# A Mamba-2 scan layer on one Trainium2 core: masked products in pairs with the decay matrix moving, and x of groups 2 and 3 turned with the last result

## The chip, the cores and the metric

The kernel runs on one core of a Trainium2 chip. The core has five engines with an instruction stream each: TensorE (PE, matrix products; its weight loads are shown apart as PEld), VectorE (DVE), ScalarE (ACT), GpSimd (POOL) and SyncE (SP, which only issues DMAs). Every engine works through its own instructions in the order of the program, and waits at semaphores for the others. The metric is the device time of one execution in microseconds (us). Before the change it is 1010.27 us, the median of three runs (1009.69 to 1010.57).

## The reference

The program is a decoder trunk of two layers for 256 tokens and a width of 1024: each layer is a SwiGLU, a token mixer and a second SwiGLU, each with a layer norm behind it. The mixer of the first layer is sparse attention, that of the second a Mamba-2 scan. Only the scan is touched:

```python
SSM_INNER = 2048; SSM_HEAD_DIM = 64; SSM_HEADS = 32; SSM_GROUPS = 4; SSM_STATE = 128; SSM_CHUNK = 128

def ssd_scan(x, dt, a, b_in, c_in):
    ...
    xdt = (x * dt[..., None]).reshape(bsz, nc, q_len, g_n, r_n, p_dim)
    a_cs = cumsum of (dt * a) within a chunk of 128 tokens
    seg = a_cs[..., :, None] - a_cs[..., None, :]
    decay = jnp.exp(jnp.where(tri, seg, -jnp.inf))
    cb = jnp.einsum('bclgn,bcsgn->bcgls', cm, bm)
    y_diag = jnp.einsum('bcgrls,bcsgrp->bclgrp', cb[:, :, :, None] * decay, xdt)
    ...
    return (y_diag + y_off).reshape(bsz, seq, n_h, p_dim)

y = ssd_scan(...) + xs * d_skip
yz = y * silu(z)                       # then an RMS norm within each group of 512 columns
return yz @ w_out
```

So there are 2 chunks (t = 0, 1) of 128 tokens, and 4 groups (g = 0 to 3) of 8 heads with 64 columns. For each chunk, group and head a 128 x 128 matrix, the product of `cb` and `decay`, is multiplied by a 128 x 64 block of `xdt`: 64 such products, the "masked products" of the title. All is float32.

## The kernel before, in words

**Weights.** All weights stream from HBM in units of 128 x 1024 numbers. Each unit is split into a high half (`wh`, a cast on ACT, lines 324 and 326) and a low half (`wl`, a subtraction on DVE, lines 351 and 354; for a few units a negative copy on ACT, line 332, and an adding DMA from POOL's queue, line 333), and a projection is three products of halves (`mm3`, lines 539 to 541). `W.pump(1)` prepares one unit further ahead, up to ten; its `wh` goes to ACT where it stands, its `wl` to DVE at the next `lows()`.

**The scan.** `ssd` runs, for g = 0 to 3, one pass of the loop over groups. The long projections stand in it as *fillers*, `f[0]`, `f[1]` and so on, which keep PE busy while the other engines work on the scan: `xs_tile` (24 products of 256 columns: x of the next group, then its convolution on ACT and DVE and a silu on ACT), `z_half` (12 products of 512 columns: half of a gate z, at its end a silu on ACT) and `out_piece` (12 products of 512 columns: the layer's output, into the four accumulator banks). Between the fillers, written out by hand in one order for all engines, stand the steps of the scan:

- `decay_load` (a DMA from POOL's queue, 512 KB), `decay_seg` (DVE), `decay_exp` (ACT, two exponentials of 1024 columns) and `decay_cb` (DVE) make M, the masked decay matrix of 8 heads, for a chunk and group.
- `x_tok` turns x of a group to tokens x columns (four transposes on PE) and multiplies it by dt and by the skip weight (two DVE instructions); `x_end` makes the block for the carry between chunks.
- `diag` does the 8 masked products of a chunk and group. M is the stationary operand, the 64 columns of x move, and the result stands as tokens x columns in a PSUM bank.
- `carry` (PE, then two DVE instructions) takes chunk 0 to chunk 1; `gate` (two DVE instructions) adds the skip part and multiplies by silu(z); `square` (ACT), `root` (POOL) and `norm` (ACT) normalise; `y_tr` turns the result back for the output projection (four transposes on PE, the high half `yH` on ACT, line 535, the low half `yL` on DVE, line 536).

ACT holds one set of function tables at a time; the exponentials need another than the silus, so each pair of `decay_exp` stands between two `ACT_TABLE_LOAD`. `late` and `flush()` put the silu of a convolution off to the next one.

**Banks.** Of PSUM's eight banks, two are called ptr, two pmm, and four (acc00, acc01, acc10, acc11) are the output's accumulators from group 2 on and lent out until then. Before the change, chunk 0's products use ptr, chunk 1's use acc11 in groups 0 and 1 and ptr in groups 2 and 3. The turned x of chunk 0 uses acc11 (pmm in group 3), that of chunk 1 uses ptr.

Of the kernel before, what the change touches and what calls it, by code (L numbers as in the profile page):

```python
# [11 lines left out]
F32 = mybir.dt.float32  # L12
# [400 lines left out]
def trunk_kernel(ctx: ExitStack, tc: tile.TileContext, widths, forms, x, ln_g, ln_b, wts, kvg, convp,  # L413
                 dt_bias, a_log, d_skip, norm_g, out):
    nc = tc.nc
# [10 lines left out]
    def nm(s):  # L426
        cnt[0] += 1
        return f"{s}_{cnt[0]}"
# [4 lines left out]
    def f2(s):  # L433
        return wk.tile([128, 512], F32, name=nm(s), tag="f2", bufs=9)
# [13 lines left out]
    def pmm():  # L448
        return psum.tile([128, 512], F32, name=nm("pmm"), tag="pmm", bufs=2)
# [11 lines left out]
    def ptr():  # L461
        return psum.tile([128, 512], F32, name=nm("ptr"), tag="ptr", bufs=2)
# [915 lines left out]
    def ssd(xT, u, ln_i):  # L1378
# [104 lines left out]
        def decay_load(t, g):  # L1483
            M[t, g] = f4("M")
            nc.gpsimd.dma_start(M[t, g], scr[t:t + 1, g * 8:(g + 1) * 8, :].rearrange("o h l -> o (h l)")
                                .to_broadcast([128, 1024]))
# [4 lines left out]
        def flush():  # L1491
            while late:
                nc.scalar.activation(*late.pop(0), AF.Silu)
# [48 lines left out]
        def decay_seg(t, g):  # L1542

            mv = M[t, g].rearrange("p (h l) -> p h l", h=8)
            nc.vector._custom_dve(TENSOR_ADD_SAT, out=mv, in0=mv, s0=0.0, s1=-3e38,
                                  in1=nacs[t][:, g * 8:(g + 1) * 8][:, :, None].to_broadcast([128, 8, 128]))

        def decay_exp(t, g):
            nc.scalar.activation(M[t, g], M[t, g], AF.Exp)
# [4 lines left out]
                                 .to_broadcast([128, 8, 128]))  # L1554

        yT = {}
        y, xd, xe, ss = {}, {}, {}, {}

        def x_tok(t, g):

            if t:
                pt = ptr()
            elif g < 3:
                pt = psum.tile([128, 512], F32, name=nm("pxt"), tag="acc11", bufs=1)
            else:
                pt = pmm()
            for i in range(4):
                nc.tensor.transpose(pt[:, i * 128:(i + 1) * 128], xsT[g][i][:, t * 128:(t + 1) * 128], ident)
            y[t], xd[t] = f2("xdt"), f2("xtok")
            nc.vector.tensor_mul(hv(y[t]), hv(pt), hb(dt[:, t * 32:(t + 1) * 32], g))  # L1570
            nc.vector.tensor_mul(hv(xd[t]), hv(pt), hb(dsk, g))
# [3 lines left out]
            nc.vector.tensor_mul(hv(xe[g]), hv(y[0]), hb(dend, g))  # L1575

        def diag(t, g):
            m = M.pop((t, g))
            py = psum.tile([128, 512], F32, name=nm("py"), tag="acc11", bufs=1) if t and g < 2 else ptr()
            for h in range(8):  # L1580
                nc.tensor.matmul(py[:, h * 64:(h + 1) * 64], m[:, h * 128:(h + 1) * 128],
                                 y[t][:, h * 64:(h + 1) * 64], start=True, stop=True)
            return py

        def carry(g):

# [5 lines left out]
        def gate(t, g, py):  # L1592
            nc.vector.tensor_add(y[t], py, xd[t])
            nc.vector.tensor_mul(y[t], y[t], zs[g][:, t * 512:(t + 1) * 512])
# [78 lines left out]
        decay_exp(1, 0)  # L1673
        W.lows()
        u += 4
        py = {}
        for g in range(SG):
            if g < 2:
                f = [lambda i=i: xs_tile(g + 1, i, u + i) for i in range(4)]
                f += [lambda t=t, i=i: (z_half(g + 2, t, i, u + 4), W.pump(1)) for t in range(2) for i in range(2)]  # L1680
            elif g == 2:
                x3 = [lambda i=i: xs_tile(3, i, u + 2 * i) for i in range(4)]
                o0 = [lambda i=i: out_piece(i, u + 2 * i + 1) for i in range(4)]
                f = [x3[0], x3[1], o0[0], x3[2], o0[1], x3[3], o0[2], o0[3]]
            else:
                f = [lambda i=i: out_piece(4 + i, u + i) for i in range(6)]
            f[0]()
            if g:
                x_tok(0, g)
                x_tok(1, g)  # L1690
            else:
                decay_cb(0, 0)
                decay_cb(1, 0)
            x_end(g)
            f[1]()
            f[2]()
            py[0] = diag(0, g)
            gate(0, g, py[0])
            carry(g)
            if g < 3:  # L1700
                decay_load(0, g + 1)
            f[3]()
            square(0)
            root(0)
            py[1] = diag(1, g)
            gate(1, g, py[1])
            if g < 3:
                decay_load(1, g + 1)
            f[4]()
            norm(0)  # L1710
            square(1)
            root(1)
            if g < 3:
                decay_seg(0, g + 1)
            f[5]()
            y_tr(0, g)
            norm(1)
            if g < 3:
                decay_seg(1, g + 1)
                f[6]()  # L1720
                flush()
                y_tr(1, g)
                decay_exp(0, g + 1)
                decay_exp(1, g + 1)
                f[7]()
                decay_cb(0, g + 1)
                decay_cb(1, g + 1)
                W.lows()
                u += 8
# [56 lines left out]
```

## Time and profile before

The page shows one profiled execution. "Busy" is the time in which an engine had an instruction running; matmuls are pipelined, so the distance between two starts is a better measure on PE than the length of one.

| | before |
|---|---|
| median of three runs | 1010.27 us |
| span of the profiled execution, first to last instruction | 1009.0 us |
| PE busy | 999.1 us (99%) |
| PEld busy | 845.8 us (84%) |
| DVE busy | 905.3 us (90%) |
| ACT busy | 662.0 us (66%) |
| POOL busy | 109.8 us (11%) |
| granted TensorE clock, mean | 0.999 |

The time of the profiled execution itself isn't listed apart from its span; the median of the runs stands 1.3 us above the span. A row of a timeline gives the start in us from the beginning of the span, the length, the engine, the line of the kernel, the operation with its output and inputs, the shape, and how many equal instructions are merged into the row. In brackets stands for how long the engine had been idle, and what ended that. A float32 product stands in the timeline as two passes, so 8 masked products are a row of 16.

### The profile page before, as it was taken

The page shows a single profiled execution, that of the slowest core. Times are in us where ns is not written, and L with a number is a line of the kernel's source. Part 1 is how long each engine was busy: PE and PEld are TensorE (multiplying, and loading weights), DVE is VectorE, ACT ScalarE, POOL GpSimd, SP SyncE. Part 2 cuts the span into 40 slices and gives each one's busy share as a digit, 9 for nine tenths or more (in the row PEclk, how much of TensorE's full clock was granted, in tenths as well). Part 3 has the DMA queues.
Part 4 walks back from the last instruction along what each step waited for, and adds up shares of the span by engine and source line. Part 5 has one row for each costly group of instructions (what it writes and reads, how often), then busy time and mean ns, then how long its engine had stood idle before and what let it go on. Part 6 is the DMA issues. An engine that isn't in the chain of part 4 may idle for free.

```text
span 1009.0 us, 14555 instructions
## 1 busy us (share of the span) xinstructions
PE 999.1 (99%) x5273; PEld 845.8 (84%) x5273; DVE 905.3 (90%) x1224; ACT 662.0 (66%) x968; POOL 109.8 (11%) x149
## 2 busy tenths in 40 slices
PE   9999999999999999999999999999999999999997
PEld 6888888898788888888888888999888888888886
DVE  7899999888898999999899998788989978899996
ACT  6676776476755767764576776486876645676670
POOL 0010110100000101100010110150221100010100
PEclk9999999999999999999999999999999999999999
DMA  9799889551754998995499889457765754699981
GB/s 347 224 289 284 240 254 334 195 172 57 245 173 126 274 280 241 260 390 183 123 281 288 243 253 357 168 179 241 222 215 181 235 191 136 170 265 285 289 254 42
DMA packets 66055, 231.69 MB, mean 230 GB/s; under 512 B 8112, under 2 KB 9136, under 8 KB 65984
## 3 DMA queue, kind: packets, MB, share of 16 engines
q1 hardware_dynamic: 54288, 189.84, 51.7%
q0 software_dynamic: 11120, 40.41, 21.7%
q8 instruction: 41, 0.67, 0.3%
q10 hardware_dynamic: 576, 0.52, 0.2%
q14 instruction: 30, 0.25, 0.1%
HBM read 193.48 MB, written 1.08 MB: 193 GB/s over the span
## 4 chain that ended last, share of the span: by engine, by line
PE 94%; DVE 3%; DMA 1%; issue 1%; POOL 0%; ACT 0%; DVEq 0%; POOLq 0%; SPq 0%
PE pmm L539 12%; PE pmm L540 12%; PE pmm L541 12%; PE acc L539 10%; PE acc L541 10%; PE acc L540 10%; PE ptr L539 2%; PE ptr L541 2%; PE ptr L540 2%; PE pxs L539 2%; PE pxs L541 2%; PE pxs L540 2%; PE pmm L705 1%; PE ptr L705 1%; PE ptr L795 1%; PE pmm L685 1%
## 5 line engine op out<-in xcount | busy, mean ns | idle before, releaser
L354 DVE TENSOR_TENSOR wl<-raw,wh 128x1024 fp32r<-128x1024 f32 (+3 forms) x424 | 495.5, 1211 | 14.6 <-ACT wh L326 14.1
L326 ACT CAST wh<-raw 128x1024 fp32r<-128x1024 f32 (+2 forms) x431 | 428.8, 1043 | 91.8 <-DVE raw L293 51.1
L539 PE MATMUL acc<-wh,hH 128*128 128x512 f32 (+1 forms) x352 | 138.1, 392 | 0.0
L541 PE MATMUL acc<-wh,hL 128*128 128x512 f32 (+1 forms) x352 | 136.5, 388 | 0.0
L540 PE MATMUL acc<-wl,hH 128*128 128x512 f32 (+1 forms) x352 | 136.3, 387 | 0.0
L539 PE MATMUL pmm<-wh,xT 128*128 128x512 f32 (+2 forms) x304 | 119.2, 392 | 0.0
L541 PE MATMUL pmm<-wh,xT 128*128 128x512 f32 (+2 forms) x304 | 116.9, 384 | 0.0
L540 PE MATMUL pmm<-wl,xT 128*128 128x512 f32 (+2 forms) x304 | 116.7, 384 | 0.1
L266 POOL DMA_DIRECT2D raw<-raw x64 | 55.8, 877 | 490.3 <-DVE raw L293 260.4
L541 PE MATMUL pmm<-wh,xf 128*128 128x512 f32 x256 | 99.6, 389 | 0.0
L539 PE MATMUL pmm<-wh,xf 128*128 128x512 f32 x256 | 99.6, 389 | 0.0
L540 PE MATMUL pmm<-wl,xf 128*128 128x512 f32 x256 | 99.6, 389 | 0.0
L541 PEld LDWEIGHTS acc<-wh,hL 128*128 128x128 f32 x352 | 66.1, 188 | 13.7
L293 DVE TENSOR_TENSOR raw<-raw,raw 128x1024 f32<-128x1024 f32 x64 | 77.0, 1218 | 0.2
L540 PEld LDWEIGHTS acc<-wl,hH 128*128 128x128 f32 x352 | 66.2, 188 | 12.9
L539 PEld LDWEIGHTS acc<-wh,hH 128*128 128x128 f32 x352 | 66.1, 188 | 12.8
L541 PEld LDWEIGHTS pmm<-wh,xT 128*128 128x128 f32 x304 | 57.0, 188 | 11.9 <-DVE xT L536 0.5
L540 PEld LDWEIGHTS pmm<-wl,xT 128*128 128x128 f32 x304 | 57.2, 188 | 11.0 <-DVE wl L354 0.8
L539 PEld LDWEIGHTS pmm<-wh,xT 128*128 128x128 f32 x304 | 57.1, 188 | 10.0
L541 PEld LDWEIGHTS pmm<-wh,xf 128*128 128x128 f32 x256 | 48.0, 188 | 10.0
L539 PEld LDWEIGHTS pmm<-wh,xf 128*128 128x128 f32 x256 | 48.0, 188 | 10.0
L540 PEld LDWEIGHTS pmm<-wl,xf 128*128 128x128 f32 x256 | 48.0, 188 | 10.0
(321 smaller groups left out, 1784.6 us busy)
## 6 DMA issues: line engine op xcount, KB each, us to landing
raw<-in_wts_dram SPq DMA_DIRECT2D x338, 512.0 KB, 5.9
raw<-raw POOLq DMA_DIRECT2D x64, 512.0 KB, 5.4
M<-scr POOLq DMA_DIRECT2D x8, 512.0 KB, 6.0
lng<-in_ln_g_dram SPq DMA_DIRECT2D x6, 512.0 KB, 5.5
lnb<-in_ln_b_dram SPq DMA_DIRECT2D x6, 512.0 KB, 5.9
wl<-raw POOLq DMA_DIRECT2D x5, 512.0 KB, 5.5
raw<-in_wts_dram SPq DMA_DIRECT2D x4, 408.0 KB, 5.4
out_dram<-x SPq DMA_DIRECT2D x4, 256.0 KB, 2.0
```

What stands on the lines that cost most here:

```text
L266: self.nc.gpsimd.dma_start(self.raw[r], self.raw[other], accum_op=ALU.add)
L293: self.nc.vector.tensor_add(self.raw[r], self.raw[r], self.raw[other])
L326: nc.scalar.copy(h[:, c:c + n], raw[:, c:c + n])
L354: self.nc.vector.tensor_sub(lo[:, s], raw[:, s], h[:, s].bitcast(F32))
L539: nc.tensor.matmul(ps, lh, rh, start=first, stop=False, skip_group_check=on)
L540: nc.tensor.matmul(ps, lh, rl, start=False, stop=False, skip_group_check=on)
L541: nc.tensor.matmul(ps, ll, rh, start=False, stop=last, skip_group_check=on)
L685: nc.tensor.matmul(ps, a, b[:, c], start=k == i == 0, stop=k == DK - 1 and i == 2)
L705: nc.tensor.matmul(ps, H[:, k * 128:(k + 1) * 128], xT.HL[:, k, :], start=k == 0, stop=False)
L795: nc.tensor.transpose(v[:, i, t * 128:(t + 1) * 128], hs[t][:, i * 128:(i + 1) * 128], ident)
```

## The change

The masked products swap their operands. The 64 columns of x become the stationary operand and M moves, 128 columns at a time; two heads are written to the two halves (partitions 0 to 63 and 64 to 127) of the same 128 columns of a bank. The result stands as columns x tokens, so ACT copies it to SBUF (`ydT`) and `back`, a new step, turns it with four transposes on PE into a ptr bank, from which `gate` reads. Between `diag` and `back` stands one filler. For that, chunk 0's `diag` goes one filler ahead in groups 1 to 3, and `gate` one filler back in group 0; chunk 1's `diag` goes ahead to stand right behind chunk 0's `back`, and the carry behind it. In group 0 the steps up to the first `y_tr` stand one filler later than before. Chunk 1's products use pmm in groups 2 and 3. The loads of the next decay matrix move ahead with the `diag` that frees their tile. `x_tok` of the next group goes to the end of the pass in groups 0 and 1 (so x of the second and third group is turned behind the last `y_tr`), and in group 0 `decay_exp` and the last filler go ahead of the second `y_tr`.

```diff
         def diag(t, g):
+
             m = M.pop((t, g))
-            py = psum.tile([128, 512], F32, name=nm("py"), tag="acc11", bufs=1) if t and g < 2 else ptr()
-            for h in range(8):
-                nc.tensor.matmul(py[:, h * 64:(h + 1) * 64], m[:, h * 128:(h + 1) * 128],
-                                 y[t][:, h * 64:(h + 1) * 64], start=True, stop=True)
+            if not t:
+                py = ptr()
+            else:
+                py = psum.tile([128, 512], F32, name=nm("py"), tag="acc11", bufs=1) if g < 2 else pmm()
+            for j in range(4):
+                for h in (2 * j, 2 * j + 1):
+                    p0 = (h % 2) * 64
+                    nc.tensor.matmul(py[p0:p0 + 64, j * 128:(j + 1) * 128], y[t][:, h * 64:(h + 1) * 64],
+                                     m[:, h * 128:(h + 1) * 128], start=True, stop=True)
+            turned[t] = f2("ydT")
+            nc.scalar.copy(turned[t], py)
+
+        def back(t):
+            a, py = turned.pop(t), ptr()
+            for j in range(4):
+                nc.tensor.transpose(py[:, j * 128:(j + 1) * 128], a[:, j * 128:(j + 1) * 128], ident)
             return py
+
+        def decay_next(t, g):
+            if g < 3:
+                decay_load(t, g + 1)
...
             f[0]()
-            if g:
+            if g == 3:
                 x_tok(0, g)
                 x_tok(1, g)
-            else:
+            if not g:
                 decay_cb(0, 0)
                 decay_cb(1, 0)
             x_end(g)
             f[1]()
-            f[2]()
-            py[0] = diag(0, g)
-            gate(0, g, py[0])
+            if g:
+                diag(0, g)
+                f[2]()
+            else:
+                f[2]()
+                diag(0, g)
+                f[3]()
+            decay_next(0, g)
+            gate(0, g, back(0))
+            diag(1, g)
+            decay_next(1, g)
             carry(g)
-            if g < 3:
-                decay_load(0, g + 1)
-            f[3]()
+            m = 4 if not g else 3
+            f[m]()
             square(0)
             root(0)
-            py[1] = diag(1, g)
-            gate(1, g, py[1])
-            if g < 3:
-                decay_load(1, g + 1)
-            f[4]()
+            gate(1, g, back(1))
+            if not g:
+                decay_seg(0, 1)
+            f[m + 1]()
             norm(0)
             square(1)
             root(1)
             if g < 3:
-                decay_seg(0, g + 1)
-            f[5]()
+                decay_seg(1 if not g else 0, g + 1)
+            f[m + 2]()
             y_tr(0, g)
             norm(1)
-            if g < 3:
+            if 0 < g < 3:
                 decay_seg(1, g + 1)
                 f[6]()
-                flush()
+            flush()
+            if g < 3:
+                if not g:
+                    decay_exp(0, 1)
+                    decay_exp(1, 1)
+                    f[7]()
                 y_tr(1, g)
-                decay_exp(0, g + 1)
-                decay_exp(1, g + 1)
-                f[7]()
+                if g:
+                    decay_exp(0, g + 1)
+                    decay_exp(1, g + 1)
+                if g < 2:
+                    x_tok(0, g + 1)
+                    x_tok(1, g + 1)
+                if g:
+                    f[7]()
                 decay_cb(0, g + 1)
                 decay_cb(1, g + 1)
                 W.lows()
```

Three places in the order of the instructions matter for what follows. Line numbers differ between the two, since the change adds lines. The first is PE in group 0, at the products of chunk 0; `ptr_7124` is their bank, `pxs` that of the filler. Before:

```order
L541 MATMUL pxs_7086<-xT_6172,wl_6760 128x256
L1581 MATMUL ptr_7124<-xdt_6990,M_6721 128x64 x8
L1588 MATMUL ptr_7135<-xe_7047,cross_6242 128x512
L539 MATMUL pxs_7141<-xT_6172,wh_6796 128x256
L540 MATMUL pxs_7141<-xT_6172,wh_6796 128x256
```

The carry (L1588) followed the products at once, and then the filler. Of the change, the products and, 24 products of the filler later, the turn back:

```order
L1587 MATMUL ptr_7124<-M_6721,xdt_6990 64x128 x8
L539 MATMUL pxs_7135<-xT_6172,wh_6796 128x256
...
L541 MATMUL pxs_7135<-xT_6172,wl_6797 128x256
L1595 MATMUL ptr_7175<-ident,ydT_7133 128x128 x4
L1587 MATMUL py_7182<-M_6723,xdt_6999 64x128 x8
L1605 MATMUL ptr_7195<-xe_7047,cross_6242 128x512
```

Chunk 1's products and the carry now follow the turn back of chunk 0. The second place is ACT at the end of group 0, from the copy `yH` of chunk 0's result on. Before:

```order
L535 CAST yH_7251<-ptr_7246 128x512
L1604 ACTIVATE xdt_6999<-xdt_6999,rs_7224 128x512
L326 CAST wh_7273<-raw_7174 128x1024
L1493 ACTIVATE xsT_7166<-cv_7167 128x256
L535 CAST yH_7282<-ptr_7277 128x512
L1549 ACT_TABLE_LOAD
L1549 ACTIVATE M_7139<-M_7139 128x1024
L1549 ACTIVATE M_7196<-M_7196 128x1024
L1479 ACT_TABLE_LOAD
L1479 ACTIVATE zs_7239<-pmm_7257 128x512
L326 CAST wh_7304<-raw_7212 128x1024
```

And now:

```order
L535 CAST yH_7285<-ptr_7280 128x512
L1621 ACTIVATE xdt_6999<-xdt_6999,rs_7258 128x512
L1493 ACTIVATE xsT_7160<-cv_7161 128x256
L1549 ACT_TABLE_LOAD
L1549 ACTIVATE M_7173<-M_7173 128x1024
L1549 ACTIVATE M_7193<-M_7193 128x1024
L1479 ACT_TABLE_LOAD
L1479 ACTIVATE zs_7246<-pmm_7261 128x512
L326 CAST wh_7309<-raw_7213 128x1024
L535 CAST yH_7317<-ptr_7312 128x512
```

The second `yH` has moved from ahead of the exponentials to behind them and behind the silu of the last filler. The third place is DVE at the same point, from the low half `yL` of chunk 1's result on. Before:

```order
L536 TENSOR_TENSOR yL_7283<-ptr_7277,yH_7282 128x512
L354 TENSOR_TENSOR wl_7274<-raw_7174,wh_7273 128x1024
L1553 TENSOR_TENSOR M_7139<-M_7139,cbm_6241 128x1024
L1553 TENSOR_TENSOR M_7196<-M_7196,cbm_6241 128x1024
L354 TENSOR_TENSOR wl_7305<-raw_7212,wh_7304 128x1024
```

And now:

```order
L536 TENSOR_TENSOR yL_7318<-ptr_7312,yH_7317 128x512
L1570 TENSOR_TENSOR xdt_7326<-pxt_7321,dt_6229 128x512
L1571 TENSOR_TENSOR xtok_7327<-pxt_7321,dsk 128x512
L1570 TENSOR_TENSOR xdt_7335<-ptr_7330,dt_6229 128x512
L1571 TENSOR_TENSOR xtok_7336<-ptr_7330,dsk 128x512
L1553 TENSOR_TENSOR M_7173<-M_7173,cbm_6241 128x1024
L1553 TENSOR_TENSOR M_7193<-M_7193,cbm_6241 128x1024
L354 TENSOR_TENSOR wl_7310<-raw_7213,wh_7309 128x1024
```

The four multiplications of the next group's x now stand between `yL` and the two masks (L1553); before, they stood behind the next group's first convolution.

More of the change, by code (lines that the diff above doesn't have):

```diff
@@ L1556, in ssd @@
         yT = {}
-        y, xd, xe, ss = {}, {}, {}, {}
+        y, xd, xe, ss, turned = {}, {}, {}, {}, {}
         def x_tok(t, g):
@@ L1675, in ssd @@
         u += 4
-        py = {}
         for g in range(SG):
```

## The prediction

> **What bounds the kernel now.** Three views, in this order. First the chain of work that ended last, on the page:
>
> ```profile
> PE 94%; DVE 3%; DMA 1%; issue 1%; POOL 0%; ACT 0%; DVEq 0%; POOLq 0%; SPq 0%
> ```
>
> TensorE (PE) carries 94% of it, so a change counts for what it does to PE's own stream. Second, the stage that is touched: the window from the first turned x of the scan to the layer's last product, by engine.
>
> ```profile
> 696.00:816.00 120.00, 119.06 (x750) 105.39 (x749) 106.10 (x139) 82.13 (x115) 18.72 (x25) 1.00 0.68 217
> ...
> 764.90 0.39 PE L540 MATMUL acc<-wl,yH 128*128 128x512 f32 x1
> 765.12 0.39 PE L541 MATMUL acc<-wh,yL 128*128 128x512 f32 x1
> 766.38 0.47 PE L539 MATMUL acc<-wh,yH 128*128 128x512 f32 x1 [0.87 <-DVE xtok L1571]
> ```
>
> The columns after the length are PE, weight load, VectorE (DVE), ScalarE (ACT) and POOL, then the granted clock, 1.00 throughout. PE is busy for 119.06 of 120 us, DVE for 106.10, ACT for 82.13: PE hardly waits, but DVE has only 14 us to spare and runs close behind it. The one real wait of PE is in the timeline below it: 1.26 us between two starts where the one before took 0.22, so 1.03 us lost, because the bank acc11 is held by the turned x of group 2 until DVE has read it. So a saving on PE is worth its full size here, as long as no new wait of PE comes up; with engines this full, that is the question. Third, therefore, the timelines of PE, ACT and DVE around the places that are changed.
>
> **The products and the turn back, on PE.**
>
> ```profile
> 737.36 0.28 PE L541 MATMUL pxs<-xT,wl 128*128 128x256 f32 x1
> 737.48 1.90 PE L1581 MATMUL ptr<-xdt,M 128*128 128x64 f32 x16
> 739.22 1.08 PE L1588 MATMUL ptr<-xe,cross 128*128 128x512 f32 x2
> 739.73 0.68 PE L539 MATMUL pxs<-xT,wh 128*128 128x256 f32 x1
> ...
> 258.22 1.09 PE L1248 MATMUL po<-pT,v 128*64 128x128 f32 x16
> 259.24 0.50 PE L539 MATMUL acc<-wh,oH 128*128 128x512 f32 x1
> ...
> 721.36 0.39 PE L541 MATMUL pmm<-wh,xT 128*128 128x512 f32 x1
> 721.59 0.60 PE L1609 MATMUL ptr<-ident,xdt 128*128 128x128 f32 x4
> 721.95 0.47 PE L539 MATMUL pmm<-wh,xT 128*128 128x512 f32 x1
> 722.26 0.39 PE L540 MATMUL pmm<-wl,xT 128*128 128x512 f32 x1
> ```
>
> Starts tell the pace. A masked product now (8 heads, 16 passes) takes 739.22 - 737.48 = 1.74 us. The new form is in this trace already: the attention's values, with a 128x64 stationary operand, 128 moving columns, and heads alternating between the two halves of the bank. Its 16 passes take 259.24 - 258.22 = 1.02 us. So each of the eight products becomes **0.72 us shorter**. Each pays for four transposes, 0.36 us (721.59 to 721.95), and the product behind them takes 0.31 instead of 0.23: **0.44 us**. Net 0.28 us, times 8: **2.2 us off PE's own work**. The carry (0.51, and 0.40 more in the 0.68 us of the product behind it: 0.9) only changes places. The moved transposes of x cost the same elsewhere; before group 2 they now stand ahead of the accumulator's first use by three fillers, so its 1.03 us wait goes. What is next there is group 2's first product, whose mask DVE has ready some microseconds earlier. **Gain so far 3.2 us.**
>
> [...]
>
> **The first wait: group 0, the copy.** A filler is one projection: 24 passes of 0.12 us (737.36 to 737.48), 2.9 us, or 12 of 0.23, 2.7 us. The copy to SBUF runs on ACT, in its order, behind what the fillers gave it.
>
> ```profile
> 707.37 2.35 DVE L1553 TENSOR_TENSOR M<-M,cbm 128x1024 f32<-128x1024 f32 x2
> 708.73 1.97 PE L1581 MATMUL ptr<-xdt,M 128*128 128x64 f32 x16
> 711.84 0.42 ACT L1493 ACTIVATE xsT<-cv 128x256 f32<-128x256 f32 x1 [0.47 <-DVE cv L1501]
> 712.16 1.03 ACT L326 CAST wh<-raw 128x1024 fp32r<-128x1024 f32 x1
> 239.57 0.59 ACT L1165 COPY kT<-pmm 128x512 f32<-128x512 f32 x1 [0.84 <-PE pmm L541]
> ```
>
> The first product still starts at 708.73. PE is then through it at 709.75 and through the filler at 712.74. ACT's order up to the cast at 712.16 is unchanged, and that cast lets the next instruction start 0.94 later, at 713.10; the copy ends at 713.69 (0.59, as the same copy at L1165), and PE can turn back at about 713.85. **PE waits 1.1 us** (between 0.8 and 1.2).
>
> Then PE runs on: turn back and second product 1.45, carry 0.9, so 716.2; filler 718.9; turn back 719.35 (DVE must have read the first turn back's bank: from the convolution that ended at 711.8 another one, a low half, a third, a low half and the addition, 1.45 + 1.13 + 1.45 + 1.13 + 0.7, make 717.7); filler 722.05; filler 724.8; transposes of y 725.2; filler 727.9; second transposes of y 728.35.
>
> **The second wait: group 1's first product.** Here the order on ACT and DVE is what counts.
>
> ```profile
> 720.88 0.63 ACT L1598 ACTIVATE xtok<-xdt 128x512 f32<-128x512 f32 x1 [1.43 <-DVE xdt L1594]
> ...
> 721.79 0.60 ACT L1479 ACTIVATE zs<-pmm 128x512 f32<-128x512 f32 x1 [0.19 <-PE pmm L541]
> 722.29 1.04 ACT L326 CAST wh<-raw 128x1024 fp32r<-128x1024 f32 x1
> 723.23 0.59 ACT L535 CAST yH<-ptr 128x512 fp32r<-128x512 f32 x1
> 723.70 0.73 ACT L1604 ACTIVATE xdt<-xdt,rs 128x512 f32<-128x512 f32 x1
> 724.33 1.05 ACT L326 CAST wh<-raw 128x1024 fp32r<-128x1024 f32 x1
> 725.26 0.43 ACT L1493 ACTIVATE xsT<-cv 128x256 f32<-128x256 f32 x1
> 725.58 0.59 ACT L535 CAST yH<-ptr 128x512 fp32r<-128x512 f32 x1
> 726.19 1.28 ACT L1549 ACT_TABLE_LOAD   x1
> 727.48 2.01 ACT L1549 ACTIVATE M<-M 128x1024 f32<-128x1024 f32 x2
> 729.51 1.28 ACT L1479 ACT_TABLE_LOAD   x1
> 730.80 0.61 ACT L1479 ACTIVATE zs<-pmm 128x512 f32<-128x512 f32 x1
> 731.30 1.04 ACT L326 CAST wh<-raw 128x1024 fp32r<-128x1024 f32 x1
> ```
>
> Before, the copy yH of the second y (725.58) runs ahead of the two exponentials and their table loads. Now, in group 0 alone, it stands behind them: table load, two exponentials, table load, silu of z, cast, and only then yH. On DVE, yL behind that yH now heads a queue: yL, four multiplications of the moved x, two by the mask (L1553). Group 1's first product needs the first mask.
>
> ACT: the silu of z starts 0.2 after the filler's end (721.59 to 721.79), so at 722.25; cast 722.75; norm 723.7; square 724.3; cast 724.95; yH of the first y 725.9. The next norm needs POOL's root, 2.8 after the start of its square (720.88 to 723.70): 727.1. Norm 0.63, silu of x 0.32, then 726.19 to 731.30 and the cast's 0.94, together 6.05: yH starts at 734.1 and ends at 734.7.
>
> ```profile
> 730.86 0.60 PE L1568 MATMUL pxt<-ident,xsT 128*128 128x128 f32 x4
> 731.65 0.36 PE L539 MATMUL pxs<-xT,wh 128*128 128x256 f32 x1
> ...
> 733.51 1.51 DVE L1501 SCALAR_TENSOR_TENSOR cv<-pxs,convp_sb,cv 128x255 f32<-128x255 f32 x3
> 734.94 0.68 DVE L1570 TENSOR_TENSOR xdt<-pxt,dt 128x512 f32<-128x512 f32 x1
> 737.33 0.68 DVE L1575 TENSOR_TENSOR xe<-xdt,dend 128x512 f32<-128x512 f32 x1
> ...
> 735.58 1.14 ACT L324 ACTIVATE wh<-raw,ng_sb 128x1024 fp32r<-128x1024 f32 x1
> ```
>
> DVE: yL 0.6, four multiplications 2.4 (734.94 to 737.33), one mask 1.22: ready at 739.0, and PE starts at 739.1, 0.14 behind the mask as at 708.73. PE is there after the transposes of x (0.8 and 0.1 behind them, 730.86 to 731.65) and two fillers of 2.9: at 735.0. **PE waits 4.1 us.** Were norm and root no hindrance, yH would come 1.4 earlier: at least 2.7; with a root slower by 0.3, 4.4.
>
> **The third and fourth wait.** While that product waits, the convolutions of group 1's first fillers wait behind the masks on DVE: second mask to 740.1, low half of a weight 1.13, convolution 1.45 (733.51 to 734.94): 742.7. ACT's order then has silu 0.32, a scaled cast 1.1, and only then the copy, 0.59: 744.7. PE has done product and filler by 739.1 + 1.02 + 0.11 + 2.88 = 743.1 and turns back at 744.85: **1.7 us** (1.2 to 2.0). From there DVE's gate comes 2.5 us behind the turn back, within the filler that PE has there, and I find no further wait but that for the last silu of x ahead of group 2's transposes, behind a cast on ACT: **0.3 us** (0 to 0.4). In groups 2 and 3 the exponentials stand behind yH as before, and copy and mask are there a microsecond or more ahead of PE.
>
> Three edits I cost at nothing. The eight copies are 8 x 0.59 = 4.7 us of ACT, which has 38 us free in the stage; what they cost is their place in the order, counted above. The moved multiplications of x are the same four on DVE. The loads of the decay matrix move ahead of the roots in POOL's queue, which helps:
>
> ```profile
> 755.99 1.23 DVE L1545 CUSTOM_DVE_ANT_1 M<-M,nacs 128x1024 f32<-128x1024 f32 x1 [2.68 <-DMA M<-scr]
> ```
>
> DVE waited 2.68 us for such a load; that ends, but it reached PE only through the bank acc11, which is counted. If a load came late all the same, DVE would have that wait back.
>
> **The sum.** Waits 1.1 + 4.1 + 1.7 + 0.3 = 7.2 us; gains 2.2 + 1.0 = 3.2 us; so 4.0 us more. The profiled execution has a span of 1009.0, the median of the runs is 1010.27, so 1.3 us lie around it: 1009.0 + 4.0 + 1.3 = **1014.3 us**, 0.4% more.
>
> **Rivals.** (1) *The waits don't come, only the work shrinks*: 1010.27 - 3.2 = **1007.1**. For it: the product itself is 0.72 us shorter without doubt, and PE had but one long wait before. It needs yH of the second y by 730.7 (735.0 less 0.14, 1.22, 2.4 and 0.6), 4 us sooner than the rows give, and the copy of group 0 by 712.6. Against it: behind y's transposes at 725.2 ACT still has two yH, a norm, a silu and the 6.05 us of loads, exponentials, silu and cast, 8.1 us in all, and ends at 733.4 even if it never waits. (2) *Smaller waits*: lower ends 0.8 + 2.7 + 1.2 = 4.7 against 3.2 to 3.6 of gain: **1011.4 to 1011.8**; for it speaks that PE's late arrival also lets casts and loads run ahead. (3) *The pairs don't overlap*, so the change doesn't do what it says: 16 passes of 128 columns at 0.11 (four transposes from 730.86 to the next four take 0.44), 1.76, so 0.74 more for each product, of which the two waits for copies swallow two: 6 x 0.74 = 4.4 more, **1018.7**. The L1248 row, same shape and order, speaks against it. (4) *DVE doesn't catch up*: it idles some 6 us for yH and has 14 in the whole stage; if group 2's copy waits behind late convolutions as group 1's does, 1.7 more: **1016.0**.
>
> **How the numbers follow.** My forecast, 1014.3 within 1012.4 and 1015.6, 0.70; (1) 0.09; (2) 0.09; (3) 0.04; (4) 0.08. The ends of all waits and gains together give 4.7 to 8.0 less 2.4 to 3.6, so 1011.4 to 1015.9; with (4) the range is 1011.0 to 1016.3. About 0.2%, 2 us, is what a measurement of this kernel tells from no change: faster 0.09, same 0.10, slower 0.81.
>
> **What would show it.** PE starts of L1587: 16 passes in about 1.0 us (else 3). In group 1 an idle of DVE of about 6 us released by ACT's yH, and of PE, some 4 us, released by DVE's mask (else 1). Waits of PE for ACT's copy ydT in group 0 and 1, of 1 to 2 us. No wait at the accumulator's first use. I am wrong if PE reaches group 1's first product and finds its mask there.

## The result and the profile after

| | before | changed |
|---|---|---|
| median of the runs | 1010.34 us (1009.69 to 1010.73, 5 runs) | 1016.07 us (1014.74 to 1016.66, 5 runs) |
| span of the profiled execution | 1009.0 us | 1014.7 us |
| start of the scan's first masked product | 708.73 us | 710.29 us |
| what is left of the span from there | 300.3 us | 304.4 us |

The changed kernel takes 1.0055 times as long (95% interval 1.0043 to 1.0067): 5.7 us more, where 4.0 were forecast. The median of 1016.07 us lies above the 1012.4 to 1015.6 us that the forecast named, and just inside the outer end of 1016.3. The last two rows of the table are the measure of all that follows, because the first masked product comes at another time in every execution, with the same code ahead of it: in the twelve traces of this study it starts between 708.7 and 710.3 us, and most of that difference is there 27 us into the program. From that product to the end, the changed kernel took 4.1 us more in these two executions.

The page's chain of waits, and the window that holds the same work as the one shown for the kernel before (from the first turned x to the layer's last product), answer to the first rows of the prediction:

```profile
PE 86%; DVE 7%; ACT 3%; DMA 2%; issue 2%; POOL 0%; SPq 0%; DVEq 0%; ACTq 0%; POOLq 0%
...
697.60:821.65 124.05, 119.71 (x782) 102.70 (x781) 106.16 (x139) 86.00 (x123) 18.22 (x25) 0.99 0.66 211
```

PE's share of the chain fell from 94% to 86%; most of what it lost went to DVE and ACT. In the window PE idles 4.3 us where it idled 0.9, and the granted clock is no longer 1.00. The timeline of PE in groups 0 and 1 shows where:

```profile
714.17 0.28 PE L541 MATMUL pxs<-xT,wl 128*128 128x256 f32 x1
715.30 0.66 PE L1595 MATMUL ptr<-ident,ydT 128*128 128x128 f32 x4 [0.84 <-ACT ydT L1590]
...
736.68 0.28 PE L541 MATMUL pxs<-xT,wl 128*128 128x256 f32 x1
740.16 1.97 PE L1587 MATMUL ptr<-M,xdt 128*64 128x128 f32 x16 [3.20 <-DVE M L1553]
742.07 0.58 PE L539 MATMUL pxs<-xT,wh 128*128 128x256 f32 x1
...
745.40 0.28 PE L541 MATMUL pxs<-xT,wl 128*128 128x256 f32 x1
745.79 0.66 PE L1595 MATMUL ptr<-ident,ydT 128*128 128x128 f32 x4
```

Each gap is read from start to start, less the 0.12 us that the pass ahead takes. The first wait is the copy of group 0: 715.30 - 714.17 - 0.12 = 1.01 us (forecast 1.1). The second is the mask of group 1: 3.36 us (forecast 4.1). The third, at the turn back of group 1, is only 0.27 us (forecast 1.7); but the product ahead of it took 1.91 us (740.16 to 742.07) instead of 1.02. ACT and DVE show the chain behind the second wait, and the copies:

```profile
730.44 2.01 ACT L1549 ACTIVATE M<-M 128x1024 f32<-128x1024 f32 x2
...
735.18 0.59 ACT L535 CAST yH<-ptr 128x512 fp32r<-128x512 f32 x1
...
745.18 0.56 ACT L1590 COPY ydT<-ptr 128x512 f32<-128x512 f32 x1
...
735.80 0.69 DVE L536 TENSOR_TENSOR yL<-ptr,yH 128x512 fp32r<-128x512 f32 x1 [5.75 <-ACT yH L535]
738.80 2.35 DVE L1553 TENSOR_TENSOR M<-M,cbm 128x1024 f32<-128x1024 f32 x2
```

The exponentials (730.44) run ahead of yH (735.18), DVE idles 5.75 us for it, and its masks come only at 738.80. The long product is explained by the windows of one to three microseconds; the column of 0.88, 0.50 and 0.92 is the granted clock:

```profile
739.00:740.00 1.00, 0.00 (x0) 0.00 (x0) 1.00 (x2) 0.00 (x0) 0.36 (x1) 0.88 0.21 41
740.00:743.00 3.00, 2.84 (x20) 2.54 (x21) 2.96 (x5) 0.00 (x0) 0.55 (x1) 0.50 0.85 161
743.00:744.00 1.00, 1.00 (x10) 1.00 (x9) 0.96 (x3) 0.19 (x1) 0.56 (x2) 0.92 0.20 45
```

With 1.00 in the microsecond ahead, a mean of 0.88 says half clock in the last 0.24 us of it, and 0.92 the same for 0.16 us: PE had been idle for about 2.8 us when its clock was halved, and it ran at 0.50 for some 3.4 us, through the whole product and a part of the filler. The prediction had nothing of this.

Last, the work itself, without waits: group 3, of the kernel before and then of the changed one. These are rows of PE's timelines, with the last projection ahead of each block and the second one behind it. The first one behind a block takes longer too, 0.3 to 0.6 us from start to start instead of 0.23, so it belongs to the cost of the block.

```profile
795.42 0.39 PE L541 MATMUL acc<-wh,yL 128*128 128x512 f32 x1
795.64 1.89 PE L1581 MATMUL ptr<-xdt,M 128*128 128x64 f32 x16
...
798.52 0.40 PE L540 MATMUL acc<-wl,yH 128*128 128x512 f32 x1
...
800.83 0.39 PE L541 MATMUL acc<-wh,yL 128*128 128x512 f32 x1
801.06 1.89 PE L1581 MATMUL ptr<-xdt,M 128*128 128x64 f32 x16
...
803.08 0.39 PE L540 MATMUL acc<-wl,yH 128*128 128x512 f32 x1
```

```profile
798.58 0.39 PE L541 MATMUL acc<-wh,yL 128*128 128x512 f32 x1
798.90 1.09 PE L1587 MATMUL ptr<-M,xdt 128*64 128x128 f32 x16
799.92 0.50 PE L539 MATMUL acc<-wh,yH 128*128 128x512 f32 x1
800.26 0.40 PE L540 MATMUL acc<-wl,yH 128*128 128x512 f32 x1
...
802.55 0.39 PE L541 MATMUL acc<-wh,yL 128*128 128x512 f32 x1
802.78 0.60 PE L1595 MATMUL ptr<-ident,ydT 128*128 128x128 f32 x4
803.31 1.09 PE L1587 MATMUL pmm<-M,xdt 128*64 128x128 f32 x16
...
805.53 0.40 PE L540 MATMUL acc<-wl,yH 128*128 128x512 f32 x1
...
807.82 0.39 PE L541 MATMUL acc<-wh,yL 128*128 128x512 f32 x1
...
808.72 0.40 PE L540 MATMUL acc<-wl,yH 128*128 128x512 f32 x1
```

From start to start of these projections, less 0.23 us for each of the two that lie in between: before 2.64 + 1.79 = 4.43 us for both products and the carry; changed 1.22 + 2.52 + 0.44 = 4.18 us with the two turns back. The gain is 0.25 us in this group, so about 1.0 us in all four, where the prediction had 2.2.

### The profile page after: what moved, and what is told of

Read it like the earlier page. It is cut to its first block, busy times and chain, and to the rows that moved or that the text cites. A ratio compares the mean times of both kernels' runs of the same rounds, so it can differ in the third digit from the quotient of the medians.

```text
span 1014.7 us, 14627 instructions
## 1 busy us (share of the span) xinstructions
PE 1000.2 (99%) x5305; PEld 842.9 (83%) x5305; DVE 905.5 (89%) x1224; ACT 666.0 (66%) x976; POOL 109.1 (11%) x149
## 4 chain that ended last, share of the span: by engine, by line
PE 86%; DVE 7%; ACT 3%; DMA 2%; issue 2%; POOL 0%; SPq 0%; DVEq 0%; ACTq 0%; POOLq 0%
PE pmm L540 12%; PE pmm L541 12%; PE pmm L539 12%; PE acc L539 9%; PE acc L541 9%; PE acc L540 9%; DVE wl L354 2%; PE ptr L539 2%; PE ptr L541 2%; PE ptr L540 2%; PE pmm L705 1%; PE ptr L705 1%; PE pxs L539 1%; PE pxs L541 1%; PE pxs L540 1%
```

## The experiments

Line numbers in the rows of a variant are its own, so a row of the same operation can carry another number. "Left" is the span that is left from the first masked product on.

| kernel | left | median | ratio to the kernel before, 95% interval |
|---|---|---|---|
| before, two traces | 300.3 and 299.3 us | 1010.2 to 1010.5 us | |
| changed, two traces | 304.4 and 305.2 us | 1016.07 and 1015.79 us | 1.0055 [1.0043, 1.0067] and 1.0054 [1.0040, 1.0067] |
| exponentials behind yH | 301.8 us | 1013.72 us | 1.0038 [1.0026, 1.0051] |
| 26 products in the wait | 305.2 us | 1016.21 us | 1.0061 [1.0047, 1.0075] |
| 13 products in the wait | 304.4 us | 1015.16 us | 1.0046 [1.0031, 1.0061] |
| copy first | 303.8 us | 1015.15 us | 1.0050 [1.0037, 1.0064] |
| same half | 307.7 us | 1018.96 us (one run) | |
| x alone, on the kernel before | 300.0 us | 1010.98 us | 1.0004 [0.9996, 1.0013] |
| both reorderings | 299.7 us | 1010.89 us | 1.0005 [0.9996, 1.0014] |
| both, and the table ahead | 298.5 us | 1009.35 us | 0.9991 [0.9982, 1.0000] |

### Does the mask wait come from the exponentials ahead of yH?

```diff
                 if not g:
-                    decay_exp(0, 1)
-                    decay_exp(1, 1)
                     f[7]()
                 y_tr(1, g)
-                if g:
-                    decay_exp(0, g + 1)
-                    decay_exp(1, g + 1)
+                decay_exp(0, g + 1)
+                decay_exp(1, g + 1)
```

> The changed kernel with one order altered: at the end of group 0 the two exponentials stand behind the copy yH of the second y on ACT, as they do at the ends of groups 1 and 2. Measure: the span that is left from the start of the first masked product on (before 1009.0 - 708.73 = 300.3 us, changed 1014.7 - 710.29 = 304.4 us). My theory (VectorE waits 5.75 us for yH because the exponentials and two table loads stand ahead of it, and TensorE waits 3.4 us for the first mask behind that): yH comes about 3 us earlier, the mask wait shrinks from 3.4 to 0.7 us (the mask is then ready at its exponential plus yL, four multiplications and 1.2 us), the granted clock stays at 1.00, and the copy behind the product keeps TensorE 1.5 to 1.7 us, since the convolutions still stand behind the masks: 301.9 us left (301.2 to 302.6). Rival (the wait comes from the four multiplications of x that now stand ahead of the masks on VectorE, not from yH): the mask is no earlier by more than 1 us, 303.4 to 304.4 us left.

301.84 us were left, as the theory said. The rows are of PE, DVE and ACT:

```profile
736.35 1.09 PE L1587 MATMUL ptr<-M,xdt 128*64 128x128 f32 x16
742.72 0.66 PE L1595 MATMUL ptr<-ident,ydT 128*128 128x128 f32 x4 [2.21 <-ACT ydT L1590]
...
731.46 0.69 DVE L536 TENSOR_TENSOR yL<-ptr,yH 128x512 fp32r<-128x512 f32 x1 [1.95 <-ACT yH L535]
...
739.44 1.28 ACT L1493 ACT_TABLE_LOAD   x1 [1.90 <-DVE cv L1501]
```

DVE's idle for yH fell from 5.75 to 1.95 us and the mask wait of 3.4 us is gone altogether, with the four multiplications of x still ahead of the masks: the rival falls. Nothing shows a halved clock: its mean over this execution is 0.998, where the changed kernel's is 0.996, and the product's row has 1.09 us instead of 1.97. The two parts of the forecast were each off, though: no mask wait where 0.7 us was expected, and 2.37 us at the copy where 1.5 to 1.7 were. That their sum came out right is luck. The last row says why the copy is later: with the exponentials last on ACT, the next silu loads its table again (1.28 us), and here that load waited together with its silu for DVE, 1.90 us.

### What does the half clock cost?

In TensorE's wait for the mask, products of the identity were put into the bank that the masked product then overwrites, so that PE is busy while it waits:

```diff
+            if not t and g == 1:
+                for i in range(26):
+                    nc.tensor.matmul(py[:, :128], ident, ident, start=True, stop=True)
             for j in range(4):
```

> The changed kernel with 26 products of the identity (about 2.9 us, results overwritten) ahead of group 1's first masked product, in TensorE's wait for the mask, so that the mask wait stays as long but TensorE isn't idle in it. My theory: the granted clock stays near 1.00 where it fell to 0.50, the masked product takes 1.0 us instead of 1.9, and nothing is won: the copy behind it on ACT is late by the convolutions on VectorE in any case, so TensorE waits 1.3 to 1.7 us there instead of 0.3, and 304.4 us are left from the first masked product on (304.2 to 304.7). Rival (the half clock costs its 0.9 us and the 0.4 us of the slowed projection): 303.1 us left (302.8 to 303.4). Second rival (the clock falls for another reason than the idle time): the product takes 1.9 us again.

This one missed: a product of the identity takes two passes of 0.113 us, the 26 took 5.89 us, and the masked product started some 2.5 us late. Still only 305.2 us were left, 0.8 more than in the first trace of the changed kernel, and PE did not wait at the turn back: there had been 1.7 us of slack behind the product. The clock's mean over the execution is 0.998. The same with 13:

> The same test as with 26 products of the identity, with 13, since one took 0.226 us (two passes) and not 0.113, so that 26 filled 5.9 us and outlasted the wait by 2.5 us. TensorE is busy for 2.9 of the 3.4 us. My theory: granted clock 1.00, masked product in 1.03 us, a wait of 1.3 to 1.7 us for the copy behind it, and 304.4 us left from the first masked product on (304.0 to 304.8, the spread of the root on GpSimd included). Rival (the half clock costs its own time): 303.1 us left (302.8 to 303.4).

PE's rows, and the granted clock (1.00) of the stretch in which it had been 0.50:

```profile
735.73 3.06 PE L1586 MATMUL ptr<-ident 128*128 128x128 f32 x26
739.09 1.09 PE L1590 MATMUL ptr<-M,xdt 128*64 128x128 f32 x16 [0.30 <-DVE M L1553]
744.72 0.66 PE L1598 MATMUL ptr<-ident,ydT 128*128 128x128 f32 x4 [1.47 <-ACT ydT L1593]
...
740.00:743.00 3.00, 3.00 (x28) 2.88 (x24) 2.93 (x6) 0.26 (x1) 1.12 (x2) 1.00 0.83 217
```

With the clock whole, the product is through in about 1 us, PE then waits for the copy (1.47 us in the row, 1.6 from start to start), and 304.4 us are left, as in the first trace of the changed kernel. From the product's start to the turn back it is 744.72 - 739.09 = 5.63 us here, and 745.79 - 740.16 = 5.63 us there at half clock. So the halved clock cost nothing in that execution: it filled the wait for the copy that the prediction had called the third. It is not always free. The control was the changed kernel, unedited:

> The changed kernel once more, without an edit, as the control of the others. If the 1.6 us by which its first masked product came later than before's is a matter of the single execution, that start lies anywhere from 708.7 to 710.3 us here; if the change causes it, again at 710.3. Left from the first masked product on: 304.4 (304.0 to 305.0).

Its first masked product started at 709.43 us, inside the range, so that start is a matter of the execution. 305.17 us were left, a little over what was expected. PE's rows and its windows, with a granted clock of 0.53 and 0.56:

```profile
739.30 1.98 PE L1587 MATMUL ptr<-M,xdt 128*64 128x128 f32 x16 [3.21 <-DVE M L1553]
745.79 0.60 PE L1595 MATMUL ptr<-ident,ydT 128*128 128x128 f32 x4
...
738.00:739.00 1.00, 0.00 (x0) 0.00 (x0) 1.00 (x2) 0.00 (x0) 0.49 (x1) 0.53 0.00 0
...
744.00:745.00 1.00, 1.00 (x7) 1.00 (x7) 0.84 (x2) 0.87 (x2) 0.00 (x0) 0.56 0.94 266
```

Here the clock was halved from about 738.1 to 744.9, twice as long. The product started at 739.30 and the turn back at 745.79, so 6.49 us: 0.86 us longer than 5.63, and by that the filler ended after the copy. The half clock cost 0.9 us in this execution and nothing in the other. The runs measured side by side with this control say something in between: the kernel with 13 products, whose trace has the whole clock, takes 1015.16 us (1014.72 to 1015.53, 4 runs), the control 1015.79 us (1015.59 to 1016.31, 4 runs), 0.6 us more, though the two ranges all but touch.

### The copy first

The first masked product of groups 0 and 1 is issued inside the filler ahead of it, between the filler's first ACT instruction and its silu:

```diff
             nc.scalar.activation(a, ps[:, :256], AF.Identity, bias=w[:, 4, i:i + 1], scale=w[:, 3, i:i + 1])
+            while between:
+                between.pop(0)()
             flush()
...
+            if g == 1:
+                between.append(lambda: diag(0, 1))
             f[1]()
-            if g:
+            if g > 1:
                 diag(0, g)
-                f[2]()
-            else:
-                f[2]()
-                diag(0, g)
-                f[3]()
+            if not g:
+                between.append(lambda: diag(0, 0))
+            f[2]()
+            if not g:
+                f[3]()
```

> The changed kernel with the first masked product of groups 0 and 1 issued inside the filler ahead of it, so that its copy stands on ACT ahead of that filler's silu and casts; TensorE's own order is the same. My theory: in group 0 the copy follows its product within 0.3 us, the wait of 1.0 us ahead of the turn back goes, and nothing is late in its place; in group 1 the copy also follows at once, but there TensorE was 0.3 us from it, so only that is won: 303.1 us left from the first masked product on (302.9 to 303.4), with the mask wait of group 1 as before (3.0 to 3.7 us) and the half clock behind it. Rival (what is won in group 0 is lost again, because the gate on VectorE stands behind the convolutions): 304.1 to 304.5 us left.

303.84 us were left, between the theory and its rival. The wait of 1.0 us in group 0 did go, and nothing came in its place there. What the theory had missed lies in group 1:

```profile
739.41 1.09 PE L1589 MATMUL ptr<-M,xdt 128*64 128x128 f32 x16 [3.82 <-DVE M L1555]
744.91 0.60 PE L1597 MATMUL ptr<-ident,ydT 128*128 128x128 f32 x4
...
740.00:741.00 1.00, 1.00 (x13) 0.83 (x10) 1.00 (x2) 0.46 (x1) 0.18 (x1) 0.81 1.04 197
741.00:744.00 3.00, 3.00 (x16) 3.00 (x16) 2.89 (x7) 1.07 (x3) 0.93 (x2) 0.50 0.84 208
```

The mask wait grew to 3.98 us between starts. PE was there 1.0 us earlier than in the first trace of the changed kernel, counted from the first masked product, and the mask only 0.4 us, mostly because ACT waited 0.51 us for the root on POOL; and with the copy early, the filler behind the product is all that stands between product and turn back. It runs at half clock, so these take 5.50 us; in the version with both reorderings, at full clock and without a wait, they take 4.00 us. Here the half clock costs its full 1.5 us.

### Why are the paired products short?

```diff
-            for j in range(4):
-                for h in (2 * j, 2 * j + 1):
-                    p0 = (h % 2) * 64
+            for h in (0, 2, 4, 6, 1, 3, 5, 7):
+                j, p0 = h // 2, (h % 2) * 64
```

> The changed kernel with the eight heads of a masked product in another order: the four that write the lower half of the bank's partitions, then the four of the upper half, so that neighbours no longer alternate between column halves of the array. Theory A (the products are short because a stationary operand of 64 columns and the moving decay matrix halve the passes' columns; alternating doesn't matter): 16 passes in 1.0 us, 304.4 us left from the first masked product on. Rival (they are short because neighbours use different column halves, and a weight load can only then lie beside running passes): 16 passes in about 1.76 us, 4.4 us more, 308.8 us left.

```profile
800.48 1.58 PE L1586 MATMUL ptr<-M,xdt 128*64 128x128 f32 x16
801.99 0.50 PE L539 MATMUL acc<-wh,yH 128*128 128x512 f32 x1
```

This kernel ran once, so the passes are read and not the time. They take 1.51 us: between the two. The passes are 0.094 us apart where neighbours write the same half of the bank's partitions, 0.064 us where they alternate, and 0.108 us in the form before. So alternating matters, by 0.5 us a product, and it is most of what the new form gains; but the form gains something without it too. Why 0.094 and not 0.11 was not tried.

### Moving x alone, and the kernel before once more

```diff
-            if g:
+            if g == 3:
                 x_tok(0, g)
                 x_tok(1, g)
...
                 decay_exp(1, g + 1)
+                if g < 2:
+                    x_tok(0, g + 1)
+                    x_tok(1, g + 1)
                 f[7]()
```

> The kernel before with one part of the change alone: x of groups 2 and 3 is turned with the last result of the group ahead, all else as before. My theory: the wait of 1.03 us at the accumulator's first use goes, the four multiplications ahead of the masks on VectorE delay no product because the masks are microseconds early there, and a wait of 0.3 us for the last silu of x comes: 299.3 to 299.6 us left from the first masked product on (before 300.3). Rival (the masks come late behind the multiplications, or the bank is then waited for elsewhere): 300.0 us or more left.

> The kernel before once more, without an edit, as control: its ratio to itself should be 1.000 within its interval. 300.3 us left from the first masked product on (300.0 to 300.6). Its first masked product starts anywhere from 708.0 to 709.5 us if the start of the program varies from run to run; the eight other traces have it at 709.0 to 710.3.

The x that moves is that of the second and third group, g = 1 and 2 of the loop; that of g = 3 stays where it was. Moving it alone won nothing that can be measured (ratio 1.0004, 299.97 us left, short of the theory by 0.4), and the reason is in the control: only 299.3 us were left there, 1.0 less than in the first trace of the same kernel and below what was expected. DVE's and PE's rows of the control:

```profile
754.00 1.22 DVE L1545 CUSTOM_DVE_ANT_1 M<-M,nacs 128x1024 f32<-128x1024 f32 x1
...
765.90 0.39 PE L541 MATMUL acc<-wh,yL 128*128 128x512 f32 x1
766.12 0.42 PE L539 MATMUL acc<-wh,yH 128*128 128x512 f32 x1
```

In the prediction's trace DVE waited 2.68 us for the load of the decay matrix ahead of this instruction and PE lost 1.03 us at the accumulator's first use. Here the load was there in time, DVE did not wait, and the accumulator's first use follows 0.22 us behind the product ahead of it. So that wait is not in every execution of the kernel; how often it comes, two traces don't say. In the variant it was absent as well, and the moved transposes cost PE 0.25 and 0.34 us, because they wait for the last silu of x.

### Both reorderings together

The two edits above, and group 1's first mask between the multiplications of the two halves of x:

```diff
                     x_tok(0, g + 1)
+                    if not g:
+                        decay_cb(0, 1)
                     x_tok(1, g + 1)
                 if g:
                     f[7]()
-                decay_cb(0, g + 1)
+                    decay_cb(0, g + 1)
                 decay_cb(1, g + 1)
```

> The changed kernel with the two reorderings on ACT together (in group 0 the exponentials behind yH; in groups 0 and 1 the copy ahead of the filler's silu and casts), and on VectorE group 1's first mask between the multiplications of the two halves of x. TensorE's order is that of the changed kernel. My theory (the three waits are all that the change lost; 301.84 us are left with the exponentials moved, and the waits for copies there are 1.07 and 2.43 us): 298.3 us left from the first masked product on (298.0 to 298.8), the clock at 1.00, no wait over 0.5 us; that is 2.0 less than before, and a time 1 to 2 us below the kernel before. Rival (VectorE doesn't catch up: a gate or a convolution behind the masks comes late and takes the place of the copies): 299.3 us or more left.

299.7 us were left: the three waits were gone, but 1.4 us came back, which is the rival's range. PE's row, the one on ACT that it may go back to, and one of DVE between them:

```profile
745.33 0.63 PE L1597 MATMUL ptr<-ident,ydT 128*128 128x128 f32 x4 [0.82 <-DVE xdt L1612]
...
738.63 1.28 ACT L1493 ACT_TABLE_LOAD   x1 [1.95 <-DVE cv L1503]
...
741.87 1.52 DVE L1503 SCALAR_TENSOR_TENSOR cv<-pxs,convp_sb,cv 128x255 f32<-128x255 f32 x3 [1.29 <-ACT cv L1498]
```

The turn back of the second product waits 1.0 us between starts for the bank that DVE's gate holds, and DVE had idled 1.29 us for ACT at the convolution ahead of that gate. Whether the gate is late by DVE's own work or by ACT's table load, through the next convolution, is told apart by loading the table earlier, with a silu of one column:

```diff
                 decay_exp(0, g + 1)
                 decay_exp(1, g + 1)
+                if not g:
+                    nc.scalar.activation(half, half, AF.Silu)
```

> The version with both reorderings, and one silu of a single column more on ACT, right behind group 0's two exponentials, so that silu's table is loaded there (1.28 us) and not ahead of group 1's first silu of x, where ACT waited for VectorE and loaded only then. My theory (of the 1.4 us that the version with both reorderings lost against its forecast of 298.3, 1.0 are the wait ahead of the turn back of group 1's second product, which comes from that table load through the silu, a cast, the next convolution and the gate on VectorE): that wait goes, and 298.3 to 298.9 us are left from the first masked product on, against 299.7 with both reorderings and 300.3 before. Rival (the gate is late by VectorE's own work, the table load lies beside it): 299.5 us or more left, with the wait in its place. Second rival (the load, now ahead of the casts of the weights, keeps a projection from starting): a new wait of TensorE of up to 1.3 us in group 1's first two fillers.

```profile
743.75 0.60 PE L1597 MATMUL ptr<-ident,ydT 128*128 128x128 f32 x4
...
732.77 1.28 ACT L1755 ACT_TABLE_LOAD   x1
```

298.5 us were left, as the theory said; the wait is gone, and no new one of that size came. It was the table load. This version takes some 6.5 us less than the changed kernel and about 1 us less than the kernel before, where the interval (0.9982 to 1.0000) reaches no change. It is the change with its long waits taken out, and so it shows how little was to be won.

## Why the prediction came out as it did

- **The time**: the forecast was 1.8 us low. The number is next to the 1016.0 of the fourth rival, but not by that rival's cause: groups 2 and 3 have no late copy.
- **The sign, and the places of the waits**: right. PE waited at the copy of group 0, at the mask of group 1 and behind it, and nowhere else for long. Putting yH ahead of the exponentials took the largest of them away, so its cause is shown.
- **The first wait**, forecast 1.1 us: measured 1.01. Issuing the copy ahead of the silu removed it.
- **The second wait**, forecast 4.1 us: measured 3.36, 3.98 in the variant with a slower root. The forecast had ACT wait 0.6 us for the root ahead of the norm; in the changed kernel's two traces ACT did not wait there, and yH came 0.5 us earlier than forecast, counted from the first masked product. The rest is PE, 0.2 us later. The lower end, "were norm and root no hindrance" 2.7, and the upper, 4.4, hold it.
- **The third wait**, forecast 1.7 us: right in place and end, though it looks otherwise. The copy did keep the turn back, by 1.6 us with PE kept busy; in the changed kernel the halved clock filled that time (0.9 us of a longer product, 0.5 us in the filler, and a wait of 0.3 us was left). In the control the half clock lasted longer and cost 0.9 us beyond the copy. That cost is missing from the sum.
- **The fourth**, forecast 0.3 us: 0.33, at group 2's x, whose eight transposes take 1.13 us from start to start where they took 0.80.
- **The pairs**, forecast 2.2 us of gain: the step that fails. The product itself was sized right (0.72 us shorter, 16 passes in 1.02 us), but by its start and end alone. With what lies around it, a first product saves 1.79 - 1.22 = 0.57 us, mostly since it starts 0.1 us later behind the projection (798.58 to 798.90 against 795.42 to 795.64). Turn back, second product and carry together save 2.64 - 2.52 = 0.12 us, where 0.72 - 0.44 = 0.28 were forecast: a turn back directly ahead of a product takes 0.53 us (802.78 to 803.31), not 0.44. The second turn back costs 0.44, as forecast. Together 0.25 us in group 3, so about 1.0 us in four groups; the version without long waits gives 1.2 us by the same measure over all four.
- **The accumulator's wait**, forecast 1.03 us of gain: taken from one trace. A second trace of the same kernel has no such wait. As a difference of the two profiled executions the term is right; as a gain of the change it counts only in executions of the kernel before that have the wait.
- **The sum**: 4.0 forecast, 4.1 in the two first traces. That these agree is in part luck: the waits came to 6.3 us (1.0 + 3.4 + 1.6 + 0.3) and not 7.2, the gains to about 2 us and not 3.2, and the two errors cancel. Against the control of the kernel before, the changed kernel's two traces lose 5.1 and 5.9 us, close to the 5.7 of the medians. So, as far as four traces go, the forecast is low by the gains, the pairs' and the accumulator's, and by the clock, and the shorter waits hide a part of that.
- **The rivals**: the waits did come (against the first); the 16 passes of a paired product take 1.02 us, not 1.76 (against the third); DVE caught up in groups 2 and 3 (against the fourth: no wait in these groups but for the silu of x).

## What to carry to other kernels

Ask of each moved or added instruction what it stands behind on its own engine, and follow that queue to the next engine that reads it: two exponentials ahead of one small copy cost more here (a wait of 3.4 us) than eight shorter products gave (about 1.0 us). Take a wait that the change is to remove from at least two executions, above all where a DMA releases it. And size a new block from the last instruction ahead of it to the second one behind it, not by its own length: the first one behind it was slowed as well, to 0.3 to 0.6 us from 0.23 in group 3.

## What the runs showed of the hardware

**The clock after a wait.** PE's granted clock fell to 0.50 in a long wait of PE or soon behind one. Read from the means of the windows as above, it was halved from about 739.8 to 743.2 in the changed kernel (3.4 us), from 738.1 to 744.9 in its control (6.8 us), and from 740.6 to 744.0 in the variant with the copy first (3.4 us). When it fell, PE had been idle for 2.8 us in the changed kernel and for 2.0 us in the control; in the variant with the copy first it had been idle for 3.8 us and had then run for 1.2 us at a clock of 1.00. A wait of 2.4 us (2.21 us idle in its row) in the variant with the exponentials behind, longer than those 2.0 us, came without a halved clock (a mean of 0.998 over that execution): the length of the wait alone does not decide, and what else does is not shown in these runs. What the half clock cost beyond the wait itself was 0, 0.9 and 1.5 us: nothing where PE had to wait for the copy in any case, all of its 1.5 us where only the filler stood between the product and the turn back.

**A table load can wait with its instruction.** ACT's load of the silu table (1.28 us) stood idle with its silu for 1.90 and 1.95 us and only then ran; a silu of one column placed earlier took it off the path in the second case, for a gain of 1.2 us.
